# Front of a hybrid attention and convolution layer: a row copy moves to VectorE, x is transposed tile by tile between zero products, one weight chunk is loaded ahead of two tiles of x, and modulation rows are turned by transposes

## The chip, the core and the metric

The kernel runs on one core of a Trainium2 chip. The metric is device time of one execution in microseconds (us). Its inputs and outputs are float32 in HBM. The core's engines, each with its own queue of instructions, are TensorE (PE in the profile; PEld is its weight load), VectorE (DVE), ScalarE (ACT), GpSimd (POOL) and SyncE (SP), which issues nearly all DMAs here.

## What is computed

One layer of an image generator on 1024 tokens (a grid of 16 rows by 64 columns), 1024 features and 256 context tokens. A conditioning vector gives shift, scale and gate; x is normalized, modulated and projected by `w_in` to eight groups of 512 columns; four feed a windowed attention with context keys, four a gated short convolution; both are gated, concatenated, projected by `w_out` and added to x. What the change touches is the first half of this:

```
def rmsnorm(x, g):
    xf = x.astype(jnp.float32)
    y = xf * lax.rsqrt(jnp.mean(xf * xf, axis=-1, keepdims=True) + RMS_EPS)
    return (y * g.astype(jnp.float32)).astype(x.dtype)

def adaln(cond, w_ada, b_ada):
    m = jax.nn.silu(cond) @ w_ada + b_ada
    return jnp.split(m, 3, axis=-1)

def hybrid_layer(...):
    shift, scale, gate = adaln(c, w_ada, b_ada)
    shift_c, scale_c, gate_c = adaln(c_ctx, w_ada, b_ada)
    h = rmsnorm(x, norm_g) * (1 + scale[:, None]) + shift[:, None]
    hc = rmsnorm(ctx, norm_g) * (1 + scale_c) + shift_c
    q, k, v, za, u, bg, cg, zc = jnp.split(h @ w_in, SPLIT_POINTS, axis=-1)
    ...
```

## The kernel before

The kernel keeps float32 accuracy by splitting each operand of a large product into a high part in TensorE's reduced format (`hh`, `wh`) and a low part (`hl`, `wl`, the difference), and by three products per block: `wh·hh`, `wl·hh`, `wh·hl`.

**The front**, which the change rewrites, turns x into `h` and does the first projection (three column groups of the first convolution block, `acc0`) as the pieces come in. x is eight tiles `xx[0..7]` of 128 tokens by 1024 features; tokens 0 to 511 are half 0, the others half 1. The features are eight slices `k`. Its helpers are:

- `load_slab(m, j)` brings 256 columns of `w_ada` (1 MB); `m` counts pairs of slices `k`, `j` is 0 for shift and 1 for scale. `load_x` brings a tile of x (512 KB), `load_chunks` a chunk of `w_in` (192 KB).
- `products(m, j)` multiplies the two conditioning vectors with a slab: eight products with two stationary columns, each of which shows as two matmuls `tr<-slab,c` in the trace. The result is two rows (four for `m` of 2 and 3, where both parts of the vectors are used).
- `row_copy(m)` brings these rows from PSUM to SBUF as `rw`; `modulation(m, rw)` turns them into columns by four small products on TensorE and then makes `ab`, shift and scale per feature, by three operations on VectorE.
- `square(xx, n)` (ACT), `root(n)` (a DVE addition, then a power on POOL) and `norm(xx, n)` (DVE) normalize a tile of x.
- `transposed(half, k)` transposes four tiles of x into one PSUM tile; `turn(half, k, on)` makes `h` from it: ACT writes the high part `h`, then ACT or DVE (`on`) the full value `hw`, then DVE the low part, `hw - h`.
- `split_chunk(k)` splits a chunk of `w_in`: ACT writes `wh`, DVE writes `wl`.
- `first_columns(half, k)` is nine products of 512 columns: three with `wh·hh`, three with `wl·hh`, three with `wh·hl`.
- `keep_clock(n)` is `n` products of a tile of zeros into `acc0[2][1]`, which is overwritten later. It was used twice, for 6 and 7 products, before the first slab is there.

`tr()` hands out PSUM tiles of one tag with two buffers. The rows of `products(m, ...)` lie in such a tile until `modulation(m)` is read out, and `transposed` takes one for each slice until `turn` has read it.

**What sets the order.** In the front all engines are chained in the order of the program's text (`strict`), SP's queue included. A DMA on SP also waits until the one eight places before it has landed, and for the release of its buffer: the slabs after the first two share three buffers, so that slab (2, 1) is issued once `products(1, 0)` has read its slab.

**After the front** (at about 75 us) come the projections of q, k, v and of the context, then the attention, with the other projections (`pu`) filling in, then the output projection. The trace gives line 55 for every instruction that passes through the chaining helper, so groups are told apart by tile names.

Of the kernel before, what the change touches and what calls it, by code (L numbers as in the profile page):

```python
# [14 lines left out]
ALU = mybir.AluOpType  # L15
# [4 lines left out]
P = 128  # L20
# [3 lines left out]
KT = D // P  # L24
# [15 lines left out]
def body(tc, es, x, ctxt, w_ada, b_ada, w_in, q_g, k_g, rpbr, w_out, vecs, cst, out):  # L40
# [70 lines left out]

    cp = es.enter_context(sbuf("cp"))
    ci = cp.tile([P, P + 2], F32, name="ci")
    ident, comb = ci[:, 0:P], ci[0:4, P:P + 2]

    vec = cp.tile([P, P], F32, name="vec")
    nvec = vecs.shape[0]
# [429 lines left out]
    load_slab(0, 1)  # L547
    load_x(range(4))
    load_chunks([0])
    load_x(range(4, 8))  # L550
    load_chunks([1])
    load_slab(1, 0)
    load_slab(1, 1)
    load_chunks([2, 3])
# [49 lines left out]
    def products(m, j, kts=range(KT)):  # L604

        if m not in mods:
            mods[m] = tr()
        rows = mods[m][:2 if m < 2 else 4, 256 * j:256 * j + 256]
        parts = [(c2, slabs[m, j])] if m < 2 else [(c4, highs[j]), (c4, lows[j])]
        for i, (c, part) in enumerate(parts):  # L610
            for kt in kts:
                pe.matmul(rows, c[:, kt], part[:, kt], start=(i == 0 and kt == 0 and j == 0),
                          stop=(i == len(parts) - 1 and kt == KT - 1 and j == 1), skip_group_check=True)

    def row_copy(m):
        n = 2 if m < 2 else 4
        rw = cvp.tile([4, 512], F32, name="rw", tag="ub", bufs=2)
        act.copy(rw[:n], mods[m][:n])
        return rw[:n]

    def modulation(m, rw):

        n, ks = 2 if m < 2 else 4, slice(2 * m, 2 * m + 2)
        pm = mods[m]
        for j in range(2):
            for i in range(2):
                pe.matmul(pm[:, 4 * j + 2 * i:4 * j + 2 * i + 2], rw[:, 256 * j + i * P:256 * j + (i + 1) * P], comb[:n],
                          start=(i == 0 and j == 0), stop=(i == 1 and j == 1), skip_group_check=True)
        both = lambda v: v[:, ks].rearrange("p (k o) -> p k o", o=1).broadcast_to([P, 2, 2])
        abk = ab[:, ks].rearrange("p k (w j) -> p j k w", w=2)  # L630
        pm = pm[:, 0:8].rearrange("p (j k w) -> p j k w", j=2, k=2)
        dve.tensor_tensor(abk[:, 0], pm[:, 0], both(bsh), ALU.add)
        dve.tensor_tensor(abk[:, 1], pm[:, 1], both(b1), ALU.add)
        dve.tensor_tensor(abk[:, 1], abk[:, 1], both(ng), ALU.mult)

    def modulated(hi, lo, ps, k, w, on):

        n = len(ps.shape) > 2 and 512 or 256
        sh, sc = (ab[:, k, 2 * w + j:2 * w + j + 1] for j in range(2))
        hw = bmp.tile([P, 512], F32, name="hw", tag="kc_s", bufs=2)  # L640
        hv = hw[:, :n]
        if n == 512:
            hv = hv.rearrange("p (r b c) -> p r b c", r=8, b=8)
        act.activation(hi, ps, AF.Identity, bias=sh, scale=sc)
        if on is act:
            act.activation(hv, ps, AF.Identity, bias=sh, scale=sc)
        else:
            dve.tensor_scalar(hv, ps, sc, sh, ALU.mult, ALU.add)
        dve.tensor_tensor(lo, hv, hi.bitcast(F32), ALU.subtract)

    def rows_of(v, half):
# [3 lines left out]
    def transposed(half, k, ts=range(4)):  # L655
        if (half, k) not in pts:
            pts[half, k] = tr()
        for i in ts:
            pe.transpose(pts[half, k][:, i * P:(i + 1) * P], xx[4 * half + i][:, k * P:(k + 1) * P], ident)

    def turn(half, k, on):

        modulated(rows_of(hh[k], half), rows_of(hl[k], half),
                  pts.pop((half, k))[:].rearrange("p (r b c) -> p r b c", r=8, b=8), k, 0, on)

    def transposed_ctx(k2):
        pts[k2] = tr()
# [55 lines left out]
    def split_chunk(k):  # L723
        chunks[k] = chunk_split(chunks[k])
# [2 lines left out]

    products(0, 0)
    products(0, 1)
    for t in range(4):  # L730
        square(xx[t], t)
    root(0)
    root(1)
    norm(xx[0], 0)
    root(2)
    norm(xx[1], 1)
    root(3)
    norm(xx[2], 2)
    rw = row_copy(0)
    modulation(0, rw)  # L740
    norm(xx[3], 3)
    transposed(0, 0)
    transposed(0, 1)
    square(xx[4], 4)
    root(4)
    split_chunk(0)
    turn(0, 0, dve)
    square(xx[5], 5)
    norm(xx[4], 4)
    root(5)  # L750
    turn(0, 1, dve)
    first_columns(0, 0)
    split_chunk(1)
    norm(xx[5], 5)
    square(xx[6], 6)
    root(6)
    square(xx[7], 7)
    norm(xx[6], 6)
    root(7)
    norm(xx[7], 7)  # L760
    first_columns(0, 1)
    products(1, 0, range(4))
    transposed(1, 0)
    turn(1, 0, act)
    products(1, 0, range(4, KT))
    load_slab(2, 1)
    load_chunks([4, 5])
    transposed(1, 1)
# [5 lines left out]
    rw = row_copy(1)  # L774
# [658 lines left out]
```

## Time and profile before

| | us |
|---|---|
| three runs: median (lowest, highest) | 649.57 (648.65, 651.94) |
| the profiled execution: its time | 650.83 |
| the profiled execution: span of the core | 649.0 |
| busy DVE | 431.1 |
| busy ACT | 322.6 |
| busy POOL | 130.1 |
| DMA, over the span | 125.46 MB, 193 GB/s |
| mean granted clock of TensorE | 0.992 |

How to read it: a time of the trace counts from the start of the span. A row of a timeline gives start, duration, engine, line, operation, `out<-in`, shapes and how many alike follow each other; the bracket gives idle time of the engine before it and what ended it. A row of windows gives for one stretch the busy time of the engines asked for, TensorE's granted clock (1.00 is full), the DMA share and GB/s. Names of tiles are those of the code; `h<-tr,ab` on ACT is the high part of `turn`, `hw` the full value, `h<-hw,h` on DVE the low part, `sqj` a square, `xss` the sums of `root`, `xx<-xx,xss` a `norm`.

### The profile page before, as it was taken

The page shows a single profiled execution, that of the slowest core. Times are in us where ns is not written, and L with a number is a line of the kernel's source. Part 1 is how long each engine was busy: PE and PEld are TensorE (multiplying, and loading weights), DVE is VectorE, ACT ScalarE, POOL GpSimd, SP SyncE. Part 2 cuts the span into 40 slices and gives each one's busy share as a digit, 9 for nine tenths or more (in the row PEclk, how much of TensorE's full clock was granted, in tenths as well). Part 3 has the DMA queues.
Part 4 walks back from the last instruction along what each step waited for, and adds up shares of the span by engine and source line. Part 5 has one row for each costly group of instructions (what it writes and reads, how often), then busy time and mean ns, then how long its engine had stood idle before and what let it go on. Part 6 is the DMA issues. An engine that isn't in the chain of part 4 may idle for free.

```text
span 649.0 us, 10300 instructions
## 1 busy us (share of the span) xinstructions
PE 631.6 (97%) x3482; PEld 542.1 (84%) x3482; DVE 431.1 (66%) x814; ACT 322.6 (50%) x693; POOL 130.1 (20%) x138
## 2 busy tenths in 40 slices
PE   7999999999999999999998999999999999999997
PEld 2577899999899999877787888888888888888885
DVE  1576756865775846458786789988998864575111
ACT  4566735533534544448676558565685644352000
POOL 2105003313223231102111111111211111004421
PEclk9799999999999999999999999999999999999999
DMA  8972656768694999799847677886862223865521
GB/s 322 321 250 97 166 177 197 212 223 232 214 288 139 270 269 237 196 238 216 215 126 195 152 171 195 208 213 155 229 168 75 74 77 115 310 236 204 197 102 49
DMA packets 118864, 125.46 MB, mean 193 GB/s; under 512 B 32817, under 2 KB 89353, under 8 KB 117532
## 3 DMA queue, kind: packets, MB, share of 16 engines
q1 hardware_dynamic: 112348, 113.23, 60.6%
q10 hardware_dynamic: 6208, 11.05, 5.4%
q8 instruction: 27, 0.44, 0.3%
q0 software_dynamic: 256, 0.54, 0.3%
q14 instruction: 25, 0.20, 0.1%
HBM read 88.01 MB, written 38.53 MB: 195 GB/s over the span
## 4 chain that ended last, share of the span: by engine, by line
PE 71%; DMA 9%; DVE 7%; ACT 5%; SPq 4%; issue 2%; POOL 1%; ACTq 0%; DVEq 0%
PE pu L55 20%; PE pacc L55 17%; PE po L55 5%; PE pout L76 4%; PE pout L75 4%; PE pout L74 4%; DMA k_s<-k_d 3%; SPq L55 3%; PE tr L55 3%; PE cacc L55 3%; PE pss L55 2%; PE acc L55 2%; PE pmx L55 2%; DVE mx L55 2%; DMA v<-v_d 2%
## 5 line engine op out<-in xcount | busy, mean ns | idle before, releaser
L55 PE MATMUL pu<-h,uh 128*128 128x512 f32 x544 | 169.0, 392 | 0.0
L55 PE MATMUL pacc<-wh,h 128*128 128x384 f32 x512 | 135.2, 338 | 0.0
L55 PEld LDWEIGHTS pu<-h,uh 128*128 128x128 f32 x544 | 98.2, 188 | 17.1
L55 PE MATMUL pu<-h,ul 128*128 128x512 f32 x272 | 106.3, 391 | 0.0
L55 PEld LDWEIGHTS pacc<-wh,h 128*128 128x128 f32 x512 | 92.8, 188 | 0.1
L55 POOL TENSOR_TENSOR plc<-sc,phc 128x512 fp32r<-128x512 f32 x32 | 42.7, 1335 | 224.1 <-ACT sc L55 88.5
L55 PE MATMUL pacc<-wl,h 128*128 128x384 f32 x256 | 85.6, 334 | 0.0
L55 POOL TENSOR_TENSOR ss<-ss,few 128x4 f32<-128x4 f32 (+1 forms) x40 | 42.0, 1051 | 127.1 <-DVE ss L55 126.7
L55 PEld LDWEIGHTS pu<-h,ul 128*128 128x128 f32 x272 | 51.1, 188 | 11.2
L55 DVE TENSOR_TENSOR mx<-mx,sb 128x384 f32<-128x384 f32 (+1 forms) x64 | 54.8, 864 | 2.0
L75 PE MATMUL pout<-wol,yh 128*128 128x512 f32 x128 | 49.8, 389 | 0.0
L76 PE MATMUL pout<-woh,yl 128*128 128x512 f32 x128 | 49.6, 389 | 0.0
L74 PE MATMUL pout<-woh,yh 128*128 128x512 f32 x128 | 48.3, 389 | 0.0
L55 PEld LDWEIGHTS pacc<-wl,h 128*128 128x128 f32 x256 | 48.1, 188 | 0.1
L55 DVE TENSOR_REDUCE ss<-sq 128x4 f32<-128x260 f32 (+1 forms) x40 | 15.7, 393 | 46.2 <-ACT sq L55 45.2
L55 ACT COPY mg<-pmx 128x256 f32<-128x256 f32 x32 | 12.0, 374 | 61.2 <-PE pmx L55 46.7
L55 ACT ACTIVATE sq<-pacc 128x256 f32<-128x256 f32 x32 | 12.3, 386 | 52.8 <-PE pacc L55 51.9
L1365 DVE TENSOR_TENSOR ot<-pout,gate 128x512 f32<-128x512 f32 x16 | 10.8, 687 | 38.6 <-PE pout L76 36.3
L55 DVE TENSOR_TENSOR pll<-sb,phl 128x768 fp32r<-128x768 f32 (+2 forms) x33 | 29.3, 889 | 8.9 <-ACT sb L55 8.9
L55 DVE TENSOR_TENSOR sc<-sc,mg 128x512 f32<-128x512 f32 x32 | 21.8, 682 | 18.4 <-ACT mg L55 18.4
L1366 POOL TENSOR_TENSOR ot<-ot,xr 128x512 f32<-128x512 f32 x15 | 20.1, 1347 | 68.2 <-DVE ot L1365 66.0
L55 ACT ACTIVATE qn<-pacc,ss 128x64 f32<-128x64 f32 x128 | 30.1, 330 | 6.5 <-POOL ss L55 3.2
(149 smaller groups left out, 1281.5 us busy)
## 6 DMA issues: line engine op xcount, KB each, us to landing
uraw<-in_w_in SPq DMA_DIRECT2D x34, 256.0 KB
q_d<-qs SPq DMA_DIRECT2D x64, 128.0 KB
k_s<-k_d SPq DMA_DIRECT2D x16, 512.0 KB
q_s<-q_d SPq DMA_DIRECT2D x32, 256.0 KB
wr<-in_w_in SPq DMA_DIRECT2D x40, 192.0 KB
slab<-in_w_ada SPq DMA_DIRECT2D x6, 1024.0 KB
t_d<-btw SPq DMA_DIRECT2D x8, 576.0 KB
bt<-t_d SPq DMA_DIRECT2D x8, 576.0 KB
```

Of the source, the lines that this page charges most:

```text
L55: i = emit(*a, **kw)
L74: i = pe.matmul(ps, ah, bh, start=first, stop=False)
L75: pe.matmul(ps, ah, bl, start=False, stop=False)
L76: pe.matmul(ps, al, bh, start=False, stop=last)
L1365: dve.tensor_tensor(ot, ps, gate[:, cols], ALU.mult)
L1366: (dve if (nh, t) == (1, NB - 1) else pool).tensor_tensor(ot, ot, xr, ALU.add)
```

## The change

It edits the front alone. The four edits that the title names, and the order that goes with them:

```
@@ loads
     load_x(range(4))
     load_chunks([0])
-    load_x(range(4, 8))
+    load_x([4, 5])
     load_chunks([1])
+    load_x([6, 7])
     load_slab(1, 0)
...
@@ def row_copy(m):
-        act.copy(rw[:n], mods[m][:n])
+        (act.copy if m else dve.tensor_copy)(rw[:n], mods[m][:n])
...
@@ def modulation(m, rw):
-                pe.matmul(pm[:, 4 * j + 2 * i:4 * j + 2 * i + 2], rw[:, 256 * j + i * P:256 * j + (i + 1) * P], comb[:n],
-                          start=(i == 0 and j == 0), stop=(i == 1 and j == 1), skip_group_check=True)
+                pe.transpose(pm[:, n * (2 * j + i):n * (2 * j + i + 1)], rw[:, 256 * j + i * P:256 * j + (i + 1) * P],
+                             ident[:n, :n])
...
+        dve.tensor_tensor(abk[:, 0], pm[:, 0, :, 0:2], both(bsh), ALU.add)
+        dve.tensor_tensor(abk[:, 1], pm[:, 1, :, 0:2], both(b1), ALU.add)
+        if n > 2:
+            for j in range(2):
+                dve.tensor_tensor(abk[:, j], abk[:, j], pm[:, j, :, 2:4], ALU.add)
...
@@ def modulated(hi, lo, ps, k, w, on, between=None):
             dve.tensor_scalar(hv, ps, sc, sh, ALU.mult, ALU.add)
+        if between:
+            between()
         dve.tensor_tensor(lo, hv, hi.bitcast(F32), ALU.subtract)
...
@@ the front
     products(0, 0)
     products(0, 1)
-    for t in range(4):
-        square(xx[t], t)
+    square(xx[0], 0)
     root(0)
+    keep_clock(2)
+    rw = row_copy(0)
+    square(xx[1], 1)
     root(1)
     norm(xx[0], 0)
+    square(xx[2], 2)
     root(2)
-    norm(xx[1], 1)
-    root(3)
-    norm(xx[2], 2)
-    rw = row_copy(0)
     modulation(0, rw)
-    norm(xx[3], 3)
-    transposed(0, 0)
-    transposed(0, 1)
+    keep_clock(2)
+    for t in range(1, 4):
+        for k in range(2):
+            transposed(0, k, [t - 1])
+        keep_clock((5, 2, 3)[t - 1])
+        norm(xx[t], t)
+        if t == 1:
+            square(xx[3], 3)
+            root(3)
+    for k in range(2):
+        transposed(0, k, [3])
+    split_chunk(0)
     square(xx[4], 4)
     root(4)
-    split_chunk(0)
     turn(0, 0, dve)
-    square(xx[5], 5)
-    norm(xx[4], 4)
-    root(5)
-    turn(0, 1, dve)
     first_columns(0, 0)
-    split_chunk(1)
-    norm(xx[5], 5)
-    square(xx[6], 6)
-    root(6)
-    square(xx[7], 7)
-    norm(xx[6], 6)
-    root(7)
+    turn(0, 1, dve, lambda: split_chunk(1))
+    for t in range(5, 8):
+        square(xx[t], t)
+        root(t)
+        norm(xx[t - 1], t - 1)
+    first_columns(0, 1)
     norm(xx[7], 7)
-    first_columns(0, 1)
-    products(1, 0, range(4))
+    products(1, 0)
     transposed(1, 0)
     turn(1, 0, act)
-    products(1, 0, range(4, KT))
     load_slab(2, 1)
```

What it does to the queues, at the three places of which the prediction speaks. The first is VectorE's queue from the first `root` to the making of `ab` for slices 0 and 1 (`xss` a step of `root`, `xx` a `norm`, `rw` the copied rows):

```order
-L55 TENSOR_SCALAR xss<-xss 128x1 x2
+L55 TENSOR_SCALAR xss<-xss 128x1
+L55 COPY rw<-tr 2x512
+L55 TENSOR_SCALAR xss<-xss 128x1
 L55 TENSOR_SCALAR xx<-xx,xss 128x1024
 L55 TENSOR_SCALAR xss<-xss 128x1
-L55 TENSOR_SCALAR xx<-xx,xss 128x1024
-L55 TENSOR_SCALAR xss<-xss 128x1
-L55 TENSOR_SCALAR xx<-xx,xss 128x1024
 L55 TENSOR_TENSOR ab<-tr,vecT 128x4
 L55 TENSOR_TENSOR ab<-tr,b_158 128x4
```

`ab` now stands behind one `norm` and three steps of `root` instead of three and four, and the copy of the rows, which was behind four squares on ACT, behind one `root`.

The second is VectorE's queue in the two `turn`s of half 0 (`wl` the low part of a chunk, `h_243` and `h_244` the slices 0 and 1 of `h`):

```order
 L55 TENSOR_SCALAR hw<-tr,ab 128x512
 L55 TENSOR_TENSOR h_243<-hw,h_243 128x8x8x8
+L55 TENSOR_SCALAR hw<-tr,ab 128x512
+L55 TENSOR_TENSOR wl<-wr,wh 128x384
+L55 TENSOR_TENSOR h_244<-hw,h_244 128x8x8x8
+L55 TENSOR_SCALAR xss<-xss 128x1
 L55 TENSOR_SCALAR xx<-xx,xss 128x1024
 L55 TENSOR_SCALAR xss<-xss 128x1
-L55 TENSOR_SCALAR hw<-tr,ab 128x512
-L55 TENSOR_TENSOR h_244<-hw,h_244 128x8x8x8
-L55 TENSOR_TENSOR wl<-wr,wh 128x384
```

A `norm` and a step of `root` have left the place between the two slices, and the chunk's low part stands ahead of the low part of slice 1.

The third is TensorE's queue behind `first_columns(0, 1)` (the `slab` rows are `products(1, 0)`, then `products(1, 1)`; the `xx` rows the transposes of half 1):

```order
 L55 MATMUL acc_215<-h_244,wh 128x512
 L55 MATMUL acc_218<-h_244,wh 128x512
-L55 MATMUL tr<-slab,c_147 2x256 x4
-L55 MATMUL tr<-ci,xx 128x128 x4
-L55 MATMUL tr<-slab,c_147 2x256 x4
-L55 MATMUL tr<-ci,xx 128x128 x4
+L55 MATMUL tr<-slab,c_147 2x256 x8
+L55 MATMUL tr<-ci,xx 128x128 x8
 L55 MATMUL tr<-slab,c_147 2x256 x8
 L55 MATMUL acc_216<-h_243,wh 128x512
```

The second half of `products(1, 0)` no longer stands between the transposes of slice 0 and those of slice 1. Behind the front the order on all engines is as before, but for the two added operations on `ab` in `modulation(2)` and `modulation(3)`.

More of the change, by code (lines that the diff above doesn't have):

```diff
@@ L113, in body @@
     ci = cp.tile([P, P + 2], F32, name="ci")
-    ident, comb = ci[:, 0:P], ci[0:4, P:P + 2]
+    ident = ci[:, 0:P]
     vec = cp.tile([P, P], F32, name="vec")
@@ L626, in modulation, with modulated @@
             for i in range(2):
-                pe.matmul(pm[:, 4 * j + 2 * i:4 * j + 2 * i + 2], rw[:, 256 * j + i * P:256 * j + (i + 1) * P], comb[:n],
-                          start=(i == 0 and j == 0), stop=(i == 1 and j == 1), skip_group_check=True)
+                pe.transpose(pm[:, n * (2 * j + i):n * (2 * j + i + 1)], rw[:, 256 * j + i * P:256 * j + (i + 1) * P],
+                             ident[:n, :n])
         both = lambda v: v[:, ks].rearrange("p (k o) -> p k o", o=1).broadcast_to([P, 2, 2])
         abk = ab[:, ks].rearrange("p k (w j) -> p j k w", w=2)
-        pm = pm[:, 0:8].rearrange("p (j k w) -> p j k w", j=2, k=2)
-        dve.tensor_tensor(abk[:, 0], pm[:, 0], both(bsh), ALU.add)
-        dve.tensor_tensor(abk[:, 1], pm[:, 1], both(b1), ALU.add)
+        pm = pm[:, 0:4 * n].rearrange("p (j k w) -> p j k w", j=2, k=2)
+        dve.tensor_tensor(abk[:, 0], pm[:, 0, :, 0:2], both(bsh), ALU.add)
[3 more added lines that the diff above has]
+                dve.tensor_tensor(abk[:, j], abk[:, j], pm[:, j, :, 2:4], ALU.add)
         dve.tensor_tensor(abk[:, 1], abk[:, 1], both(ng), ALU.mult)
-    def modulated(hi, lo, ps, k, w, on):
+    def modulated(hi, lo, ps, k, w, on, between=None):
         n = len(ps.shape) > 2 and 512 or 256
@@ L659, in transposed, with turn @@
             pe.transpose(pts[half, k][:, i * P:(i + 1) * P], xx[4 * half + i][:, k * P:(k + 1) * P], ident)
-    def turn(half, k, on):
+    def turn(half, k, on, between=None):
         modulated(rows_of(hh[k], half), rows_of(hl[k], half),
-                  pts.pop((half, k))[:].rearrange("p (r b c) -> p r b c", r=8, b=8), k, 0, on)
+                  pts.pop((half, k))[:].rearrange("p (r b c) -> p r b c", r=8, b=8), k, 0, on, between)
     def transposed_ctx(k2):
```

## The prediction

> **What bounds the kernel now.** I read the busy times first, by stretches of the span. Columns: busy time of PE, PEld, DVE, ACT and POOL, granted clock, DMA share, GB/s.
>
> ```profile
> 17.97:24.80 6.83, 6.20 (x17) 4.73 (x18) 5.91 (x12) 5.15 (x10) 1.28 (x2) 0.50 1.07 387
> 24.80:60.00 35.20, 34.84 (x195) 24.23 (x194) 21.96 (x33) 20.37 (x28) 4.62 (x6) 1.00 0.62 208
> 60.00:110.00 50.00, 49.85 (x304) 44.98 (x302) 31.15 (x66) 26.18 (x61) 10.99 (x14) 1.00 0.55 165
> 110.00:649.00 539.00, 527.50 (x2913) 462.71 (x2913) 368.32 (x693) 262.68 (x583) 108.80 (x107) 1.00 0.67 188
> ```
>
> From 24.8 us on TensorE has hardly a gap, and the change leaves its order there as it was. So the change is worth what it moves the start of this dense work, unless a later wait takes some of it back. Before it TensorE waits, and then runs at half the clock. Its own timeline shows both:
>
> ```profile
> 16.27 1.05 PE L55 MATMUL tr<-ci,rw 2*128 2x2 f32 x8 [3.25 <-ACT rw L55]
> 17.25 0.55 PE L55 MATMUL tr<-ci,xx 128*128 128x128 f32 x3
> 18.59 1.33 PE L55 MATMUL tr<-ci,xx 128*128 128x128 f32 x5 [0.78 <-DVE xss L55]
> 19.93 1.65 PE L55 MATMUL acc<-h,wh 128*128 128x512 f32 x3
> 21.38 1.48 PE L55 MATMUL acc<-h,wl 128*128 128x512 f32 x3
> 22.66 2.54 PE L55 MATMUL acc<-h,wh 128*128 128x512 f32 x6
> 25.04 0.85 PE L55 MATMUL acc<-h,wl 128*128 128x512 f32 x3
> 25.72 0.84 PE L55 MATMUL acc<-h,wh 128*128 128x512 f32 x3
> 26.50 1.89 PE L55 MATMUL tr<-slab,c 128*2 128x256 f32 x8
> 28.31 0.66 PE L55 MATMUL tr<-ci,xx 128*128 128x128 f32 x4
> 28.90 1.89 PE L55 MATMUL tr<-slab,c 128*2 128x256 f32 x8
> 30.72 0.66 PE L55 MATMUL tr<-ci,xx 128*128 128x128 f32 x4
> ```
>
> The first slabs' products end at 16.27 - 3.25 = 13.02; the 18 products of `first_columns` take 19.93 to 26.50, 6.57 us. Three of them start 0.68 apart from the next three at full clock (25.04, 25.72) and 1.28 at half (21.38, 22.66). From 28.31 on no row shows a gap, and the two halves of `products(1, 0)` stand around the first transposes of half 1. Next, what the first products wait for, on VectorE, POOL and ACT:
>
> ```profile
> 17.43 0.16 DVE L55 TENSOR_TENSOR ab<-tr,vecT 128x4 f32<-128x4 f32 x1 [0.81 <-PE tr L55]
> ...
> 17.78 0.75 DVE L55 TENSOR_SCALAR xx<-xx,xss 128x1024 f32<-128x1024 f32 x1
> ...
> 19.91 0.81 DVE L55 TENSOR_SCALAR hw<-tr,ab 128x512 f32<-128x512 f32 x1 [0.85 <-ACT h L55]
> 20.76 0.69 DVE L55 TENSOR_TENSOR h<-hw,h 128x512 fp32r<-128x512 f32 x1
> ...
> 23.54 0.55 DVE L55 TENSOR_TENSOR wl<-wr,wh 128x384 fp32r<-128x384 f32 x1
> ```
>
> ```profile
> 16.02 1.01 POOL L55 TENSOR_TENSOR xss<-xss,few 128x1 f32<-128x1 f32 x1 [0.21 <-DVE xss L55]
> ```
>
> ```profile
> 19.10 0.78 ACT L55 ACTIVATE h<-tr,ab 128x512 fp32r<-128x512 f32 x1 [1.07 <-PE tr L55]
> ...
> 29.01 0.78 ACT L55 ACTIVATE h<-tr,ab 128x512 fp32r<-128x512 f32 x1 [4.79 <-PE tr L55]
> 29.69 0.77 ACT L55 ACTIVATE hw<-tr,ab 128x512 f32<-128x512 f32 x1
> ```
>
> POOL's result for `xx[3]` is there at 17.03, but its `norm` starts at 17.78: it stands behind `ab`, which stands behind the row copy, which stands behind four squares.
>
> **The change, part by part.**
>
> *The row copy* on VectorE takes between 0.55 (its `wl`, 384 columns) and 0.81 us (its `hw`, 512 columns out of PSUM); I take 0.65, nearest the second but for two partitions. From 13.05 the rows are there by 13.9, four transposes later (at most the 1.05 of the old form) `ab` can start at 14.6 to 14.9. Behind the copy stand `root(1)`, the first `norm` and everything for half 0, but POOL needs 1.01 us per power, four in a row, and the last power can't start before the square of `xx[3]`, as now: it ends at 17.03 again. So the copy costs nothing within its bounds (0.2 at the upper one, if the second `norm` slips), and the last `norm` starts at 17.05, 0.73 us earlier. Transposes of `xx[3]` then start at 17.86 instead of 18.59. ACT's `h`, which needs the first of them, came 0.51 behind it at half clock; at full clock I take 0.3: 18.17 instead of 19.10, and the first product 0.83 later, as now: 19.0 instead of 19.93.
>
> *The zero products* are 14 at some 0.23 us (0.68 / 3, the nearest row), 3.2 us between 13.02 and 17.86, where TensorE has nothing but 10 short transposes. They cost nothing if the last three end by 17.86; behind the transposes of `xx[2]` at about 16.9 they end at 17.7. If a group runs over, the products slip by the same, at most 0.7 us. What they can buy is the clock. Columns: PE busy, clock, DMA share, GB/s.
>
> ```profile
> 11.15:14.56 3.41, 1.87 (x9) 1.00 1.04 406
> 14.56:17.97 3.41, 1.53 (x11) 1.00 1.03 422
> 352.48:355.89 3.41, 1.70 (x9) 1.00 0.50 131
> 355.89:359.31 3.42, 3.42 (x16) 0.50 0.27 77
> ```
>
> Both half-clock stretches (17.97 to 24.80, 355.89 to 359.31) come behind a stretch of 3.41 us in which TensorE was busy for 1.53 and 1.70; behind 1.87 the clock stayed. With the zero products 14.56 to 17.97 has some 2.4 us of products plus transposes, above all three. I take full clock.
>
> *`first_columns`*: at full clock the 18 would take 18 x 0.227 = 4.1 us; the data set a little more. `hw` of slice 0 waits for ACT's `h` (as at 19.91): 18.98; low part 19.82 to 20.51 (spacing 0.85 and 0.61 as now); `hw` of slice 1 from 20.43, the chunk's low part at 21.2 to 21.75, low part of slice 1 to 22.35. Products: 19.00, 19.7, 20.56 (waits for the low part), 21.25, 21.95, 22.65, end at 23.35. That is 3.15 us earlier than 26.50. In the middle `norm`s of half 1 have been pushed back; the last is done at about 26.3 by four powers of 1.01 in a row from 22.4, used at 27.0.
>
> *The loads*: the order of chunk 1 and two tiles changes, the sum ahead of slab (1, 0) does not. When that slab is there SP's queue tells:
>
> ```profile
> SPq L55 <- PE tr L55: 7.4, 1, 7.4
> SPq L55 <- DMA slab<-in_w_ada: 0.5, 1, 0.5
> ```
>
> SP waited 0.5 us for the slab, then 7.4 us for TensorE's last product with it (28.90 + 1.89 = 30.79), so the slab landed at 23.4. `products(1, 0)` can't start earlier, now or then: **23.4**, a gain of 3.1 and its upper bound. Back from there at 387 GB/s (1.05 MB, 0.52 MB a tile), `xx[7]` is there at 20.7 and chunk 1 at 18.0; they are needed at 22.4 and 19.6. The moved chunk costs nothing.
>
> *`products(1, 0)` in one piece* gives half of it back. 16 matmuls at (30.72 - 28.90) / 8 = 0.228 end at 27.05; then the transposes of slice 0. Those of slice 1 need the PSUM tile that ACT's `hw` releases (30.46 now, 2.15 us behind the start of the first transposes at 28.31). Now 1.82 us of products cover that; then nothing does: the second transposes start at 27.05 + 2.15 = 29.2, after **1.5 us of idle TensorE**, and 30.72 - 29.2 = **1.5 us** is the gain from here on. `products(1, 1)` and the rest follow in the old order.
>
> *The transposes for the rows* replace eight matmuls by four, in `modulation(1)` to `(3)`:
>
> ```profile
> 66.14 1.05 PE L55 MATMUL tr<-ci,rw 4*128 4x2 f32 x8
> ...
> 69.51 1.06 ACT L55 CAST wh<-wr 128x384 fp32r<-128x384 f32 x2 [2.10 <-DMA wr<-in_w_in]
> ```
>
> The four transposes of 128 columns above took 0.59 to the next row (28.31, 28.90), the eight small ones 0.98 (16.27, 17.25): a saving of 0.4 to 0.5, taken as 0.45; zero if a transpose of a row costs as two matmuls. Two of the three move the path. Behind the third ACT stands waiting for a DMA at 69.51, with the next `h` for TensorE behind it, so that one is lost. The two added operations on `ab` are 0.2 us of VectorE (0.16 each, overlapped), with no product waiting for them in the dense stretch; were their cover gone, 0.2.
>
> *What takes it back later.* One wait in the projections:
>
> ```profile
> 110.98 0.33 PE L55 MATMUL trA<-ci,rot 128*128 128x128 f32 x1 [1.08 <-DVE rot L55]
> ```
>
> It hangs on work of DVE, POOL and SP that starts behind the front's last slabs, which move with TensorE up to `modulation(2)`. I let it grow by what `modulation(3)` saves and no more.
>
> **Sum**: 1.5 + 2 x 0.45 = 2.4 us. The profiled execution took 650.83 (span 649.0 and 1.8 around it), so it becomes 648.4. It lies 1.26 above the median shown, 649.57, to which I apply the same: **647.2 us**, 0.4% less.
>
> **Rivals.**
>
> *More comes through.* The second half-clock stretch follows this gap of TensorE:
>
> ```profile
> 355.18 0.30 PE L55 MATMUL pmx<-ci,mx 128*128 128x128 f32 x1 [1.51 <-DVE mx L55]
> ```
>
> It starts at 353.67. Moved by 2.4 us against the steps of 3.41 us, it falls on both sides of 352.48, and neither step has under 1.87 busy. A stretch of 3.42 at half clock costs up to 1.7; I take 1.2. With half of the third saving: 649.57 - 2.4 - 1.4 = 645.8. Against it: the three runs may not all have had that stretch.
>
> *The zero products don't hold the clock.* Then 18 products run from 19.0 at 0.43 (1.28 / 3) until 24.8, which is 13, and five at 0.227: 26.0, only 0.5 earlier than now; the lost cover costs 1.55, the transposes give 0.9: 649.6 + 0.2 = 649.8. For it: 17.25 to 19.93 TensorE was mostly busy and the clock did not come back. Against it: the numbers above.
>
> *Slower: the uncovered wait halves the clock.* Place: 27.05 to 29.8, 1.5 us idle between two sets of four transposes. If the transposes don't count as work, 2.75 of a step of 3.41 are empty, more than the 1.88 and 1.71 that sufficed above; if they count, 3.41 - 1.5 = 1.91 are busy, just over the 1.87 that held. The price is half of the half-clock stretch of dense work: 3.4 us for two steps as at 17.97, so 649.57 - 2.4 + 3.4 = 650.6; it decides from 4.8 us of half clock. The Trainium skill, "TensorE: Matmul & The Clock Gate", Part 4, says that transposes don't count as busy in the same way, which speaks for this rival; by it the time would be this 650.6. No row here separates the two.
>
> **How the numbers follow.** Chances: forecast 0.45 (its own range 646.0 to 648.6); more comes through 0.30; clock not held 0.09; wait halves the clock 0.12; something worse, the last two together, 0.04 (about 653). A measurement here tells a change from none at about 0.5%, 3.2 us, so faster means under 646.3: most of the 0.30 and a quarter of the forecast, 0.39; slower means over 652.8: 0.05; same 0.56. Range for 8 in 10: 644.9, below the second case with the full 1.7, to 650.2, which takes in the third and stops short of the fourth.
>
> **What would show it.** Right: the copy of `rw` on DVE at 13.1; first `acc` product near 19.0 at clock 1.00; the first `slab` product behind them at 23.4; a gap of 1.5 us before the second set of `xx` transposes, ended by ACT `hw`; four `tr<-ci,rw` matmuls per modulation. Wrong: a granted clock of 0.50 anywhere between 18 and 35; first `acc` later than 19.5; `slab` products later than 24; no gap at the transposes; a wait at about 109 grown by 1 us or more, which would eat the gain.

## The result, and the profile after

The change makes the kernel 0.4% faster: 646.88 us (median of eight runs, 645.63 to 648.0) against 649.09 us for the kernel before on the same chip (eight runs, 648.46 to 651.94). The ratio is 0.9959, 95% interval 0.9943 to 0.9976, so 1.6 to 3.7 us are gained. The forecast was 647.2 us, and its sum said 2.4 us. The profiled execution took 646.57 us (span 644.8).

The windows of the kernel after; columns: busy time of PE, PEld, DVE, ACT and POOL, granted clock, DMA share, GB/s.

```profile
17.97:24.80 6.83, 6.02 (x26) 3.68 (x24) 5.71 (x12) 5.20 (x9) 2.14 (x3) 1.00 1.06 393
24.80:60.00 35.20, 33.25 (x191) 23.21 (x189) 24.10 (x37) 22.23 (x31) 6.14 (x7) 1.00 0.62 207
60.00:110.00 50.00, 48.12 (x289) 42.96 (x288) 30.88 (x70) 25.46 (x63) 9.28 (x13) 1.00 0.58 171
```

The first stretch ran at half the clock before and holds 26 matmuls now instead of 17, some of them zero products. The second has 1.95 us without TensorE work, where it had 0.36: that is the price. (The third has 1.88 instead of 0.15, above all because the wait ahead of `trA`, transposes in the projections, now falls before 110.) TensorE's timeline of the kernel after, at the places that the prediction shows of before:

```profile
18.50 0.44 PE L55 MATMUL tr<-ci,xx 128*128 128x128 f32 x2
19.70 0.96 PE L55 MATMUL acc<-h,wh 128*128 128x512 f32 x3 [0.76 <-ACT h L55]
...
24.23 3.62 PE L55 MATMUL tr<-slab,c 128*2 128x256 f32 x16
27.77 0.65 PE L55 MATMUL tr<-ci,xx 128*128 128x128 f32 x4
29.96 0.66 PE L55 MATMUL tr<-ci,xx 128*128 128x128 f32 x4 [1.54 <-ACT hw L55]
...
36.82 0.40 PE L55 MATMUL tr<-ci,rw 2*128 2x2 f32 x4
37.15 0.95 PE L55 MATMUL acc<-h,wh 128*128 128x512 f32 x3
...
64.14 0.41 PE L55 MATMUL tr<-ci,rw 4*128 4x4 f32 x4
...
69.47 0.99 PE L55 MATMUL acc<-h,wh 128*128 128x512 f32 x3 [0.38 <-ACT h L55]
...
109.80 0.33 PE L55 MATMUL trA<-ci,rot 128*128 128x128 f32 x1 [1.42 <-DVE rot L55]
```

Read against the rows of before, it gives the gain along the path: 0.23 us at the first product (19.93 to 19.70), 2.27 at the products with slab (1, 0) (26.50 to 24.23), 0.76 at the second transposes of half 1 (30.72 to 29.96), 2.00 at `modulation(3)` (66.14 to 64.14), 1.18 at `trA` (110.98 to 109.80). So most of it is made in `first_columns`, two thirds of that are lost within 6 us, the row transposes bring some back, and 0.8 us go between 64 and 110. Behind 110 the trace of before lost more time of its own (its half-clock stretch at 355.89); that is taken up below.

VectorE, then POOL, of the kernel after:

```profile
13.81 0.68 DVE L55 COPY rw<-tr 2x512 f32<-2x512 f32 x1 [1.44 <-PE tr L55]
14.42 0.13 DVE L55 TENSOR_SCALAR xss<-xss 128x1 f32<-128x1 f32 x1
...
17.69 0.75 DVE L55 TENSOR_SCALAR xx<-xx,xss 128x1024 f32<-128x1024 f32 x1 [0.44 <-POOL xss L55]
```

```profile
14.63 3.03 POOL L55 TENSOR_TENSOR xss<-xss,few 128x1 f32<-128x1 f32 x3 [1.54 <-DVE xss L55]
```

The copy runs from 13.81 on, because the first slabs' products ended at 13.77 in this execution (13.02 in that of before). `root(1)` (the addition at 14.42) comes behind it, and the last three powers then follow each other on POOL until 17.66, where the last `norm` waits for them.

Windows of the kernel after, PE alone:

```profile
11.15:14.56 3.41, 3.18 (x16) 1.00 1.06 411
14.56:17.97 3.41, 3.25 (x20) 1.00 1.04 405
...
352.48:355.89 3.41, 3.35 (x23) 1.00 0.10 27
```

The zero products fill the stretches that had 1.87 and 1.53 us of work. The thin stretch ahead of 355.89, which came from a gap of 1.51 us, did not occur here.

### The profile page after: what moved, and what is told of

It reads as the page before. It is cut to its first block, busy times and chain, and to the rows that moved or that the text cites. A ratio compares the mean times of both kernels' runs of the same rounds, so it can differ in the third digit from the quotient of the medians.

```text
span 644.8 us, 10300 instructions
## 1 busy us (share of the span) xinstructions
PE 629.4 (98%) x3479; PEld 537.3 (83%) x3480; DVE 432.9 (67%) x819; ACT 322.2 (50%) x692; POOL 130.3 (20%) x138
## 4 chain that ended last, share of the span: by engine, by line
PE 68%; DMA 9%; DVE 8%; ACT 6%; SPq 5%; issue 2%; POOL 2%; ACTq 0%; DVEq 0%; POOLq 0%
PE pu L55 18%; PE pacc L55 17%; PE po L55 5%; PE pout L76 5%; PE pout L75 5%; PE pout L74 4%; DMA v<-v_d 3%; DMA k_s<-k_d 3%; PE tr L55 3%; SPq L55 3%; PE cacc L55 3%; DVE mx L55 2%; PE acc L55 2%; PE pss L55 2%; PE pmx L55 2%
```

## The experiments

All were timed in five rounds beside the kernel before. Runs of one group (I, II, III) ran on the same chip and share the runs of the kernel before (medians 648.71, 649.58 and 649.85 us). e1 has seven runs, the others have twelve. The clock is the median over the timed runs of the mean clock granted in a run; 0.001 of it is 1.3 us at half clock, or 0.65 us of work.

| run | what | us (lowest, highest) | ratio (95%) | clock |
|---|---|---|---|---|
| e0_after (I) | the changed kernel again | 646.54 (645.34, 648.57) | 0.9959 (0.9941, 0.9976) | 1.000 |
| e0_before (III) | the kernel before again | 648.64 (646.11, 651.86) | 0.9980 (0.9958, 1.0003) | 0.9935 |
| e1_split (I) | after, `products(1, 0)` in halves again | 645.83 (644.82, 646.57) | 0.9950 (0.9928, 0.9971) | 1.000 |
| e2_rows (I) | before, with the row transposes alone | 648.15 (644.62, 652.88) | 0.9991 (0.9967, 1.0015) | 0.994 |
| e3_nozero (I) | after, without the zero products | 648.80 (646.93, 652.52) | 1.0000 (0.9984, 1.0017) | 0.994 |
| e5_loads (II) | after, with the old order of loads | 647.82 (645.03, 650.15) | 0.9973 (0.9954, 0.9992) | 0.999 |
| e6_norows (II) | after, without the row transposes | 648.68 (645.81, 650.21) | 0.9984 (0.9968, 0.9999) | 0.999 |
| e8_bzeros (II) | before, with the zero products alone | 649.21 (647.85, 652.21) | 0.9998 (0.9978, 1.0018) | 0.997 |
| e9_best (II) | e1, with `root(1)` ahead of the copy | 645.71 (644.48, 650.24) | 0.9948 (0.9927, 0.9969) | 0.9995 |
| e4_actcopy (III) | after, the row copy back on ACT | 648.23 (646.53, 650.3) | 0.9972 (0.9952, 0.9992) | 0.999 |
| e7_together (III) | after, half 0 transposed together | 646.48 (643.49, 647.91) | 0.9945 (0.9926, 0.9964) | 0.999 |
| e10_gains (III) | e1, with work of POOL moved back | 648.74 (647.01, 651.39) | 0.9990 (0.9967, 1.0013) | 0.999 |

**The two kernels again.**

> The changed kernel once more, beside the three others and with a second profile. Both theories of the others: ratio to before 0.995 to 0.997. In the profile: a gap of 1.5 us before the second set of transposes of half 1 again, clock 1.00 from 18 to 35 if the products of zeros hold it wherever the clock's steps fall. If the gap of TensorE at 354 and the half clock behind it in the trace of before come with that kernel's order, they are absent again; if they come and go with the execution, they may be there.

> The kernel before once more, with a second profile. Theory A (its first profile fell into a bad stretch near 354: a gap of TensorE of 1.5 us and half the clock behind it, which the nine other profiles don't have, and x early): no such gap, TensorE's end 642 to 643.5 instead of 644.56, while the front is as it was, half the clock for 6.8 us around 18 to 25 and no gap before the second transposes of half 1. Theory B (the gap at 354 belongs to its order): it is there again. The ratio is 1.000 by both.

The changed kernel repeats its ratio. The kernel before comes out 0.2% from itself, with an interval that just holds 1: differences of that size between runs of this table mean nothing.

Their traces say how much of the profiles shown first is chance. Three lines of PE's timeline of the kernel before, second trace:

```profile
21.38 1.65 PE L55 MATMUL acc<-h,wh 128*128 128x512 f32 x3
...
27.91 1.89 PE L55 MATMUL tr<-slab,c 128*2 128x256 f32 x8
...
113.14 0.33 PE L55 MATMUL trA<-ci,rot 128*128 128x128 f32 x1 [1.41 <-DVE rot L55]
```

Here the first product starts at 21.38, not 19.93, and `trA` at 113.14, not 110.98. The first tile of x was there at 10.80 in the first trace (ACT's first square starts) and at 11.44 in this one; over the 14 traces between 10.80 and 12.67. Times below are therefore also given from x: first product minus first square. That is 9.13 and 9.94 us before, 8.66 and 8.29 after. The two other kernels with the old order have 8.50 (e2) and 8.93 (e8), and one with the new order has 9.27 (e10), so from x the two ranges overlap. Over both traces `trA` comes at 112.06 us before and 109.86 after, 2.2 us apart like the medians of the runs. And no gap stands at 354 in the second trace.

**e1_split: is the lost cover worth 1.5 us?**

```
-    products(1, 0)
+    products(1, 0, range(4))
     transposed(1, 0)
     turn(1, 0, act)
+    products(1, 0, range(4, KT))
```

> The changed kernel with products(1, 0) cut in two halves again, around the transposes of half 1's slice 0, as before the change. In the changed kernel's trace TensorE is idle for 1.54 us before the second set of transposes, until ACT's hw is done. Theory A (that wait is uncovered path): the gap is under 0.1 us, the second set of transposes starts at 28.4 to 28.6 instead of 29.96, and everything up to the wait at 109.8 is 1.4 to 1.5 us earlier than in the changed kernel; the time is 1.0 to 1.5 us under the changed kernel's (ratio to before 0.994). Theory B (the start of the dense work is not what sets the end, since the work on DVE, POOL and SP behind the wait at 109.8 starts from something else): the gap goes, but the wait at 109.8 grows from 1.4 to nearly 3 us and the time is that of the changed kernel (ratio 0.996).

PE's timeline of e1:

```profile
24.44 1.89 PE L55 MATMUL tr<-slab,c 128*2 128x256 f32 x8
26.26 0.55 PE L55 MATMUL tr<-ci,xx 128*128 128x128 f32 x3
27.01 0.33 PE L55 MATMUL tr<-ci,xx 128*128 128x128 f32 x1 [0.20 <-DVE xx L55]
27.27 1.89 PE L55 MATMUL tr<-slab,c 128*2 128x256 f32 x8
29.09 0.66 PE L55 MATMUL tr<-ci,xx 128*128 128x128 f32 x4
```

From the first slab product to the second transposes it takes 4.65 us, 5.73 in the kernel after, 4.22 before. The wait for `hw` is gone, and 0.2 us of waiting for the last `norm` (x7) has come in its place, the step that the prediction gave as done by about 26.3 and needed at 27.0. `trA` comes at 108.63, 1.2 us before that of the changed kernel; in the runs 0.7 us show, and the intervals overlap.

**e3_nozero: do the zero products hold the clock?** The three calls `keep_clock(2)`, `keep_clock(2)` and `keep_clock((5, 2, 3)[t - 1])` are taken out of the changed kernel.

> The changed kernel without the 14 products of zeros (it computes the same). Theory A (they hold the clock): the granted clock is 0.50 for 3.4 or 6.8 us from about 18, first_columns takes 5.5 to 6.5 us instead of 4.5, and TensorE is 1 to 2 us later than in the changed kernel from 28 us on; ratio to before 0.997 to 1.000. Theory B (transposes tile by tile alone keep TensorE busy enough, or the data of the turns set the pace anyway): clock 1.00 or a delay under 0.4 us, ratio 0.996 as the changed kernel.

Windows of e3, PE alone:

```profile
12.31:15.73 3.42, 2.17 (x12) 1.00 1.04 404
15.73:19.14 3.41, 1.44 (x7) 1.00 1.05 407
19.14:22.55 3.41, 2.92 (x7) 0.50 1.06 392
22.55:30.00 7.45, 6.94 (x33) 1.00 1.01 348
```

The step with 1.44 us of work is followed by half clock, just where `first_columns` starts (19.63): it takes 5.66 us instead of 4.53, and the time is that of the kernel before. This execution is a mild case: its mean clock is 0.997, which is one step at half clock, and the median of the runs is 0.994, about two. So the 1.1 us lost here can be no more than a part of the 2.3 us by which the runs are slower than e0_after. All of the gain goes; the interval lies clear of that of the changed kernel on the same chip. The clocks of the timed runs say the same without a trace: of 91 runs of the eight kernels with the change's zero products (e0_after, e1, e4 to e7, e9, e10) 88 have 0.997 or more, of 100 runs of the kernel before 2 have 0.996 or more, and the 12 of e3 lie at 0.991 to 0.997.

**e8_bzeros: is the clock enough?** In the kernel before, 15 zero products at two places:

```
     products(0, 1)
+    keep_clock(12)
...
-    transposed(0, 0)
+    transposed(0, 0, range(3))
+    keep_clock(3)
+    transposed(0, 0, [3])
```

> The kernel before with products of zeros alone added: 12 behind the first slabs' products, where TensorE idles 3.25 us, and 3 between the transposes of xx[2] and xx[3]. Theory A (the clock is the larger part of the gain, since without the zeros the changed kernel was as slow as before): clock 1.00 from 18 on, the slab products 0.8 to 1.2 us earlier than the 26.50 of before (the data of turn(0, 1) hold them until about 25.5), and no new gap, so the ratio is 0.997 to 0.9985. Theory B (the clock is worth nothing without the earlier data): ratio 1.000, slab products at 26.3 or later.

PE's timeline of e8:

```profile
20.84 0.96 PE L55 MATMUL acc<-h,wh 128*128 128x512 f32 x3 [0.43 <-ACT h L55]
...
25.05 0.98 PE L55 MATMUL acc<-h,wl 128*128 128x512 f32 x3 [0.98 <-DVE wl L55]
...
26.65 1.89 PE L55 MATMUL tr<-slab,c 128*2 128x256 f32 x8
```

The clock is held in the trace (1.00 from 18 on). Over the runs it is 0.997 in the median, so in the middle run about one step at half clock is left somewhere; the four runs with 0.999 or more took 647.85 to 652.21 us, no less than the others. The time is not told from before. Part of what the clock brings turns into a wait for the chunk's low part, which in the old order stands behind more of VectorE's work: from the first product to the slab's it takes 5.81 us, against 6.57 before and 4.53 after. With e3 it makes a cross: clock alone 0.9998, the new order (with all other edits) alone 1.0000, both 0.9959. By the medians each is of use only with the other. The intervals leave room for 1.4 us (e8) and 1.0 us (e3) by each alone, so the cross speaks for it and does not prove it. Which part of the new order shortens `first_columns` from 5.81 to 4.53 us was not run alone.

**e2_rows and e6_norows: the row transposes.** e2 puts the new `modulation` into the kernel before, e6 the old one into the kernel after, with its sums for `ab`. The core of e6, of which e2 is the reverse:

```
-                pe.transpose(pm[:, n * (2 * j + i):n * (2 * j + i + 1)], rw[...], ident[:n, :n])
+                pe.matmul(pm[:, 4 * j + 2 * i:4 * j + 2 * i + 2], rw[...], comb[:n],
+                          start=(i == 0 and j == 0), stop=(i == 1 and j == 1), skip_group_check=True)
```

> The kernel before with the row transposes alone (four transposes in place of eight matmuls per modulation, two more operations on VectorE in the last two). Theory A: each modulation saves 0.6 us of TensorE, as the two traces show (0.98 to 0.33 between the first small matmul and the next row); two of them move the path: TensorE is 1.2 to 1.4 us earlier behind modulation(2), some of it is lost at the wait at 111, and the time is 0.7 to 1.3 us under before (ratio 0.998 to 0.999). Theory B: the gain of the change is all from the rewritten start, and the saved TensorE time is lost in later waits: ratio 1.000.

> The changed kernel with the old products in modulation (eight matmuls each, two operations fewer on VectorE in the last two). Theory A (two savings of 0.6 us reach the path): TensorE is 0.6 us later than in the changed kernel behind modulation(1), 1.2 us behind modulation(2), POOL's first rg is 1.2 us later at the same start of the second transposes, and the time is 0.8 to 1.3 us over the changed kernel's (ratio to before 0.9975). Theory B (it is absorbed by later waits): ratio 0.996.

PE's timeline of e6:

```profile
36.51 1.05 PE L55 MATMUL tr<-ci,rw 2*128 2x2 f32 x8
37.48 0.73 PE L55 MATMUL acc<-h,wh 128*128 128x512 f32 x2
```

To the next product it takes 0.97 us with the eight matmuls and 0.33 with the four transposes (36.82 to 37.15 in the kernel after): 0.64 each. From `modulation(1)` to `(2)` it is 13.60 us in e6 and 13.03 after, from `(2)` to `(3)` 14.92 and 14.29; so two of them come through. Behind the third, 0.38 us of waiting for ACT takes most of it (69.47 above). The two are still there at `trA`: from `modulation(1)` to it e6 takes 74.00 us, the kernel after 72.98 and 72.63 in its two traces, so 1.0 to 1.4 us less. (Between the two traces of before the same stretch differs by 0.75.) In the runs e6 is 2.1 us slower than e0_after, with overlapping intervals and on another chip; e2 is not told from the kernel before. The trace shows the term, the times alone would not.

**e7_together: do the transposes tile by tile matter?** The zero products stay; the eight transposes of half 0 stand together behind the last `norm`.

```
-        for k in range(2):
-            transposed(0, k, [t - 1])
         keep_clock((5, 2, 3)[t - 1])
...
     for k in range(2):
-        transposed(0, k, [3])
+        transposed(0, k)
```

> The changed kernel with the eight transposes of half 0 in one piece behind the norm of xx[3], slice by slice as before the change; the 14 products of zeros stay. Theory A (only the transposes of xx[3] have to come last; the others were off the path, and slice 0's h waits for four transposes instead of one): first acc product 0.3 to 0.4 us later than in the changed kernel behind the same arrival of x, products(1, 0) later by the same, time up 0.2 to 0.4 us, ratio 0.9962 to 0.9966. Theory B (without transposes between them the zeros leave longer gaps and the clock falls): clock 0.50 behind 18, ratio 0.998 to 1.000.

PE's timeline of e7:

```profile
16.77 0.59 PE L55 MATMUL tr<-ci,xx 128*128 128x128 f32 x3
18.22 0.76 PE L55 MATMUL tr<-ci,xx 128*128 128x128 f32 x5 [0.87 <-DVE xx L55]
19.42 0.96 PE L55 MATMUL acc<-h,wh 128*128 128x512 f32 x3 [0.43 <-ACT h L55]
```

TensorE comes to the last tile's transposes in time as well, and the first four, which ACT needs, come first. The first product is 8.28 us behind x, as in the kernel after (8.29 and 8.66), and the ratio is 0.9945. That edit of the change is worth nothing that shows here; the loss that one theory expected of taking it out did not come.

**e4_actcopy and e5_loads: the copy's engine and the order of loads.** e4 has `act.copy(rw[:n], mods[m][:n])` for every `m`; e5 goes back to `load_x(range(4, 8))` ahead of `load_chunks([1])`.

> The changed kernel with the first rows copied on ACT, in the place where VectorE copies them now: behind the square of xx[0] and ahead of that of xx[1]. Theory A (the copy has to leave ACT, whose squares are paced by the arrival of x): the copy can't run before 13 to 13.8, so the squares of xx[1] to xx[3] start at 14.3 or later and run back to back, the norm of xx[3] starts 1.0 to 1.6 us later, first acc at 20.7 to 21.2, products(1, 0) 1.0 to 1.5 us later, ratio 0.998. Theory B (POOL's three powers of 1 us set that norm, wherever the copy is): first acc within 0.4 us of the changed kernel's, ratio 0.996.

> The changed kernel with the loads in the old order, chunk 1 behind x6 and x7. Theory A (chunk 1 is then late): it lands at about 20.8 instead of 18; ACT's wh of chunk 1 waits until 20.9 to 21.1 and with it, in order, the squares of half 1; the products of wl of chunk 1 start 0.5 to 0.8 us later; products(1, 0), which could start with its slab at 23.5 to 23.7, starts 0.3 to 0.8 us later than in the changed kernel, time up by as much (ratio 0.9965 to 0.997). Theory B (the slab is the later one anyway): the slab products start when they did, 24.2 to 24.7, ratio 0.996.

In e4 the first product comes 8.70 us behind x, where e5, e6 and e7, in which x also came late against the first slab's products, have 8.26 to 8.30: in these traces the copy between ACT's squares costs 0.4 us. In e5 ACT does wait for the chunk, as its timeline shows:

```profile
22.25 0.52 ACT L55 CAST wh<-wr 128x384 fp32r<-128x384 f32 x1 [0.96 <-DMA wr<-in_w_in]
```

but `first_columns` takes 4.51 us all the same. Both ratios (0.9972 and 0.9973) lie between those of before and after, and their intervals overlap the latter's: in the times neither edit is told from nothing.

**e9_best: the copy behind the squares' roots.** In e1, `rw = row_copy(0)` moves behind `root(1)`.

> The changed kernel with products(1, 0) in two halves (as in the run e1_split) and with root(1) ahead of the row copy on VectorE instead of behind it. In the changed kernel's trace the copy (13.81 to 14.49) holds back root(1), whose square was done at 13.5, and POOL then makes the last three powers without a break, 14.63 to 17.66, so that the norm of xx[3] starts at 17.69. Theory A (POOL's chain of powers sets the first product, and the copy on VectorE is what delayed it): the second power starts by 13.8, the norm of xx[3] at 17.0 to 17.2, the first acc product 0.5 to 0.7 us earlier than in e1_split (19.0 to 19.2), the slab products 0.4 to 0.6 us earlier, and the time 0.3 to 0.6 us under e1_split's 645.83. Theory B (the arrival of x sets it): first acc at 19.7 again, same time as e1_split.

The first product comes 8.37 us behind x (e1: 8.30), and the ratio is that of e1. So here the arrival of x set it, not the copy. But x was late in this trace (12.67), and the first slabs' products had begun early for it (7.44). The traces with the copy on VectorE ahead of `root(1)` show two floors, of which the later one holds:

| trace | first slab product + 13.0 | first square + 8.28 | first `acc` product |
|---|---|---|---|
| after | 6.70: 19.70 | 11.04: 19.32 | 19.70 |
| e0_after | 7.17: 20.17 | 11.87: 20.15 | 20.16 |
| e1 | 6.71: 19.71 | 11.41: 19.69 | 19.71 |
| e3 | 6.50: 19.50 | 11.32: 19.60 | 19.63 |
| e5 | 5.95: 18.95 | 12.37: 20.65 | 20.67 |
| e6 | 5.87: 18.87 | 11.14: 19.42 | 19.40 |
| e7 | 5.99: 18.99 | 11.14: 19.42 | 19.42 |
| e10 | 7.44: 20.44 | 11.16: 19.44 | 20.43 |

The two constants are taken from `after` and e7, and the other six agree to 0.03 us. The first floor is the one that runs through the copy, `root(1)` and three powers (13.77 to 17.69 in the kernel after). It holds in `after` and in e10, where it costs 0.4 and 1.0 us.

What moves this floor is not the slab, for which the first of those products waits in no trace. It is the seven zero products ahead of them, which the kernel had before the change. They take between 1.68 and 3.17 us; in the kernel before, then in e10:

```profile
4.34 1.68 PE L55 MATMUL acc<-warm 128*128 128x512 bf16 x7
```

```profile
4.34 3.17 PE L55 MATMUL acc<-warm 128*128 128x512 bf16 x7
```

That is 0.24 and 0.45 us each, near the spacing of the products of `first_columns` at full clock (0.23) and at half (0.43). The first record of the full clock lies at 4.32 and 7.41 us in these two traces and between 4.03 and 7.41 in all 14, and the later it lies, the longer the seven take. So the copy costs something in those executions in which the clock rises late against the arrival of x.

e9's order should lower it; in e9 itself that floor did not hold, so this stays untried. The wait for x7's `norm` stays, 0.41 us in e9.

**e10_gains: what the wait at `trA` hangs on.** In e1, `gkc = gains(tables)`, which makes POOL's `rg`, moves behind the second `norm` of the context's tile.

> The run e1_split with gains(tables), POOL's four rg operations of 1.5 us each and the store behind them, placed behind the normalization of the context instead of ahead of it; four chunk loads on SP then no longer wait for that store. Theory A (the wait of TensorE near 109 hangs on POOL's rg, through the chunk loads and SP's queue): POOL's powers come 6 us earlier, the chunk loads are issued 2 us or more earlier (62 to 64 in the changed kernel), ACT no longer waits for a chunk near 67, the first of the 24 bias table DMAs is issued 0.7 to 2 us earlier than in e1_split (71.05), and the wait of 1.4 us near 108 shrinks by as much; time 0.5 to 1.2 us under e1_split, ratio 0.993 to 0.9945. Theory B (SP's queue is paced by TensorE's own work in the last turns, through the release of the chunks' buffers): the bias tables are issued at 71 again and nothing is gained, ratio 0.995.

SyncE's queue around the store of `rg`, in e1 and then in e10 (start, time until the next, what is issued):

```profile
61.14 0.33 SPq L55 DMA_DIRECT2D rope_d<-rg  x1
61.52 9.48 SPq L55 DMA_DIRECT2D wr<-in_w_in  x8
71.05 5.45 SPq L55 DMA_DIRECT2D t_d<-in_rpb  x8
```

```profile
62.84 0.37 SPq L55 DMA_DIRECT2D wr<-in_w_in  x1
68.85 0.34 SPq L55 DMA_DIRECT2D rope_d<-rg  x1
69.28 3.36 SPq L55 DMA_DIRECT2D wr<-in_w_in  x4
72.69 5.45 SPq L55 DMA_DIRECT2D t_d<-in_rpb  x8
```

`rg` starts at 62.96 instead of 55.16, its store waits for it until 68.85, and SP holds the chunks and the bias tables behind it: the tables are issued 1.64 us later, `trA` comes 1.76 us later (110.39 against 108.63), and the ratio goes from 0.995 to 0.999. Neither theory expected a loss. The second half of the link shows: `trA` follows the first table by 37.58 us in e1 and by 37.70 in e10, so the tables' place in SP's queue is the path to it, and TensorE's own wait there hardly changes (1.37 and 1.40). How much of the delay is due to `rg` does not show, since e10 was already 0.72 us late at the second transposes of half 1 (29.81 against 29.09), and in its trace the chain to the tables runs over VectorE's split of a chunk (until 72.10) and not over `rg`, as it does in e1.

## Why the prediction was right, step by step

- **First product at 19.0: near from x, late from the span's start (19.70 and 20.16).** It and the slab's products (24.23 and 24.69) lie beyond 19.5 and 24, the prediction's own signs of being wrong; those limits counted from the span's start. Forecast was 8.2 us behind x (19.0 - 10.80); after has 8.66 and 8.29, the others with its copy 8.26 to 8.37, but for e10 (9.27). The start of 10.80, from one trace, was the earliest of 14. The copy's cost was put at 0 to 0.2. It is 0.4 and 1.0 where the first slabs' products come late against x: a copy at 13.81 instead of the assumed 13.05 moves `root(1)` and with it three powers in a row. The step took the start of the first slab's products and the arrival of x in one trace for fixed.
- **Full clock: right**, on its own condition. Both stretches that were named have over 3 us of work and the clock is 1.00; without the zero products (e3) it halves. The clock's own steps fall elsewhere in each execution: in the kernel after they are 12.73 to 16.14 and 16.14 to 19.55, with 3.02 and 2.75 us of work, so the zero products were enough there too. The rival "not held" fell; its sum for that case, a time 0.2 us above that of before, is what e3 measured (1.0000). What the prediction did not say is that the clock would be worth as little without the data (e8).
- **`first_columns` in 4.35 us: 4.53** in both traces.
- **Slab products at 23.4, set by the slab: 24.23 and 24.69.** By SP's queue the slab landed at 23.68 in the trace after and at 24.43 in e0_after, so the 23.4 was not the same in each execution; with the later first product TensorE became the later one. So 2.27 us of the 3.1 showed in the first pair of traces, and 3.22 in the second (27.91 to 24.69).
- **1.5 us of idle TensorE: 1.54**, ended by ACT's `hw`, in each of the seven traces of kernels with `products(1, 0)` in one piece, and gone in e1.
- **0.45 per row transpose, two carried: 0.6 each, two carried**, and most of the third lost at ACT's `h`, as said.
- **A wait at 110 grown by 0.45: by 0.34 in the first pair of traces**, from 1.08 to 1.42, **and by 0.02 in the second**, from 1.41 to 1.43. That it grew is therefore not shown. In the first pair another 0.48 us goes between 69 and 108.
- **The rival with more gain** needs the gap at 354 in the runs of before. It was in the first trace of the kernel before (1.51 us, then half clock) and, smaller and with the clock kept, in e5 (1.08 us), in none of the other twelve. It belongs to an execution, not to the order of before, and that profiled execution lay 1.7 us above the median. Here the shift of the sum by 1.26 us from the profile to the median was the right call.
- **The slower rival, half clock by the uncovered wait, fell** in all seven traces with the gap; why is shown in the last section. It had set 2.75 us of empty time, transposes left out, beside 1.88 and 1.71 us, in which transposes count as work.

The sum of 2.4 us stands against 2.2. Its terms erred both ways: a first product 0.1 to 0.5 late from x, against 0.3 more from the two row transposes. That it meets the medians so closely is in part luck: its first term, 1.5 us at the second transposes of half 1, is 0.76 in the first pair of traces and 1.71 in the second (32.14 to 30.43), and at `trA` the two pairs have 1.18 and 3.23.

Of the parts of the change that were taken out one by one, the times single out only the zero products (e3). The row transposes show in the traces; the copy's engine shows there once, with 0.4 us (e4); the transposes tile by tile and the order of loads show nothing of use.

Of the versions tried, `products(1, 0)` in halves (e1, e9) and the transposes together (e7) have the lowest ratios, 0.9945 to 0.9950. They are not told from each other or, by their intervals, from the changed kernel. In the trace the halves are worth 1.2 us at `trA`, so by the traces the change with that one edit undone is the version to keep.

## What to carry to other kernels

Here filler work for the clock paid only where the engine was then held by its own rate; where it then waited for data, both had to move together, and each alone could not be told from nothing (to about 0.2%). Before a block of work is put in one piece, ask which wait its second half was covering: here 1.54 us, half to two thirds of what had been won up to there. Measure times from the arrival of the first data, not from the start of the trace, and take a second trace of the kernel before: arrival moved by 1.9 us between executions, nearly as much as the whole effect.

## What the runs showed of the hardware

**How much work holds the clock.** The clock changes on steps of 3.41 us; the half-clock stretches were of one, two and three steps (3.41, 6.83 and 10.24 us). The three of the kernel before's second trace (windows, PE alone):

```profile
5.66:15.90 10.24, 8.00 (x37) 1.00 1.05 403
15.90:26.14 10.24, 8.78 (x27) 0.50 1.07 390
```

Set out by the work in the step, transposes counted, the traces give one order:

| work in a step of 3.41 us | kernel, step | the next step |
|---|---|---|
| 0.41 | e2, 14.29 to 17.70 | half |
| 1.17 | before, second trace, 12.49 to 15.90 | half |
| 1.44 | e3, 15.73 to 19.14 | half |
| 1.53 | before, 14.56 to 17.97 | half |
| 1.70 | before, 352.48 to 355.89 | half |
| 1.87 | before, 11.15 to 14.56 | full |
| 1.87 | e0_after, 27.31 to 30.72 | full |
| 1.87 | e5, 28.21 to 31.62 | full |
| 2.05 | after, 26.38 to 29.79 | full |

The last three steps hold the uncovered wait. Their place is counted on in steps from the first record of the clock (6.83, 4.31 and 5.90 us), since no change of clock marks them.

**Transposes counted as work for keeping the clock.** The window of e0_after, PE alone, then the same for the products with the slab only:

```profile
27.31:30.72 3.41, 1.87 (x12) 1.00 0.95 307
```

```profile
27.31:30.72 3.41, 0.99 (x5) 1.00 0.95 307
```

In the kernel before's second trace, a window of products with the slab alone, without a transpose:

```profile
12.49:15.90 3.41, 1.17 (x6) 1.00 1.05 408
```

Without the transposes 0.99 us are left in e0_after (0.70 in e5), less than the 1.17 that halved the clock in the kernel before; it stayed at 1.00. (The 1.46 left in the kernel after do not decide it.) The Trainium skill, "TensorE: Matmul & The Clock Gate", Part 4, says that a transpose doesn't count as busy in the same way. For keeping the clock these runs do not agree with it. For getting it back they do. In e2 the first step at half clock has 2.92 us of work, 2.10 of them transposes:

```profile
17.71:21.12 3.41, 2.92 (x10) 0.50 1.05 393
```

The next step stayed at half. In e3 the same 2.92 us at half clock, without a transpose, restored it (19.14 to 22.55). The kernel before agrees with e2: 2.79 us, 1.33 of them transposes, did not restore it (17.97 to 21.39).
